# Where the causal mask is added in two attention groups, and how group A's low-order keys are laid out

## The chip, the cores and the metric

The kernel runs as one program on one core of a Trainium2 chip. The core has a matrix engine (TensorE, PE in the profile, with its weight loads as PEld), a vector engine (VectorE, DVE), an activation engine (ScalarE, ACT), GpSimd (POOL) and a queue that starts transfers (SyncE, SP). Each engine works through its own list of instructions in order and waits on semaphores of the others. Matrix products land in PSUM, which the kernel holds as eight tiles of 128 by 512 float32. The metric is device time in microseconds (us), the median of several runs; lower is better.

## The reference

One decoder layer over 512 tokens of width 2048: RMSNorm, one input projection, three token mixers side by side (A: differential attention, B: a gated linear recurrence, C: sparse attention with compressed, selected and window branches), one output projection, then a SwiGLU feed-forward and a last norm. The change touches the scores of A and of two branches of C.

```python
# A: 4 heads, 2 components of 64 dimensions each, causal
s = jnp.einsum('bqhcd,bkhcd->bhcqk', qi, k) * scale
p = masked_softmax(s, kpos[None, :] <= qpos[:, None])
pd = p[:, :, 0] - lam * p[:, :, 1]
...
# C: 6 heads of 128 dimensions; at 512 tokens the selected branch takes every block
s = jnp.einsum('bqgjd,bgqnld->bgjqnl', qi, ksel) * scale
p = masked_softmax(s, mask)
...
s_w = jnp.einsum('bnqgjd,bnkgd->bgjnqk', qw, kwb) * scale
p_w = masked_softmax(s_w, jnp.asarray((dist >= 0) & (dist < WINDOW)))
```

`masked_softmax` puts minus infinity where the mask is false, subtracts the row's maximum, exponentiates and divides by the sum.

## The kernel before

Every float32 operand of a large product is split into a high part rounded to TensorE's fast float32 form ("hi") and the rest ("lo"); a product is then hi·hi + hi·lo + lo·hi, three matrix products into one PSUM tile. ScalarE makes hi (L202) and VectorE makes lo (L203) of each weight tile `w`, from a tile `raw` that SyncE fetched.

The attention runs inside the projections. `tick` counts the time that projection products should take and, each time a set amount has passed (2560 ns during group C, 3840 ns during group A), takes one step of the attention that is queued in a "lane". TensorE's order is exactly the order in which the code is written; the orders of VectorE, ScalarE and GpSimd come from a list scheduler with an estimate of its own. Group C's attention (`c_attention`, 617 to 790 us of the span) lies between projections `paq`, `pak` and `pav`; group A's (`a_attention`, 820 to 925 us) between products `po` of the output projection.

`pipeline` lays the attention out in steps. A step takes one unit: it issues the unit's scores, then the transposes `pt` of the unit before, whose softmax has to be ready by then, then the products with the values of the unit before that. In C a unit is a head, a block of 128 queries and one or two branches (6 units a head, 36 in all); in A it is a head and a block (4 a head, 16 in all), always with both components. Between a unit's scores and its transposes stands one step of projection products, some twelve.

The scores of C are three hi/lo products into a tile `cs` (keys `kh`, `kl`; queries `cqh`, `cql`) and, for each branch, a bfloat16 product of the identity with the mask tile `causal`, which adds a large negative number above the diagonal of the last 128 columns. Then VectorE takes the negated row maximum (`nm`, L916), ScalarE the exponential with its sum (`pr`, `z`, L922), and VectorE the reciprocal and the scaling of `pr` (L925 to L930). In A each component has a tile `as`. Its 64 dimensions are packed so that one product of 128 rows gives hi·hi and lo·hi together: `aqs` holds the query's hi in the component's own 64 rows and its lo in the other 64, `aks` the key's hi twice. The key's lo, `akl`, is one tile for both components, each in its own 64 rows, so the second product has only 64 rows; the third is the mask (all through `mm`, L145). VectorE takes the maximum (L1033), ScalarE the exponential (L1035), and VectorE combines both components (L1037 to L1041).

`a_split(h)` makes these tiles for a head (ScalarE L1001 and L1002, GpSimd L1003, VectorE L1004 and L1005), one head ahead. `at` tiles are a ring of three PSUM tiles, shared by scores, transposes and `finish`, which transposes a finished head of A into `ayp`; a new `at` tile waits until its predecessor three tiles back has been read. `x<-x,po` (L1090) adds a finished column block of the output projection to the residual.

Of the kernel before, what the change touches and what calls it, by code (L numbers as in the profile page):

```python
# [31 lines left out]
F32 = mybir.dt.float32  # L32
F32R = mybir.dt.float32r
BF16 = mybir.dt.bfloat16
I32 = mybir.dt.int32
AF = mybir.ActivationFunctionType
ALU = mybir.AluOpType
# [3 lines left out]
P = 128  # L41
T = 512
# [21 lines left out]
C_MASK = C_D + N_D  # L64
# [43 lines left out]
def tile_hymba(ctx: ExitStack, tc: tile.TileContext, x, attn_norm, w_in, q1, k1, q2, k2, da_norm, hg_norm,  # L108
# [3 lines left out]
    pe, act, dve, pool, sp = nc.tensor, nc.scalar, nc.vector, nc.gpsimd, nc.sync  # L112
# [31 lines left out]
    def mm(o, l, r, start, stop, **kw):  # L144
        return pe.matmul(o, l, r, start=start, stop=stop, **kw)  # L145
# [195 lines left out]
    with ExitStack() as p1:  # L341
# [72 lines left out]
        with tc.manual_schedule(engines=others):  # L414
            g = [pj(f"g1{q}") for q in range(4)]
            for q in range(4):
                mm(g[q], ones, grow[q // 2][:, (q % 2) * 512:(q % 2 + 1) * 512], True, True)

            def take_gain(hf):
                for q in (2 * hf, 2 * hf + 1):  # L420
                    dve.tensor_copy(gain1[:, q * 512:(q + 1) * 512], g[q])

            hn = prepare_x(0, take_gain)
            split_w0(range(12), pool)
            ps0 = [pj(f"pf0{j}") for j in range(2)]
            for tt in range(NT):
                for b in range(4):
                    to_d_major(tt, b, hn, hT)
                if tt == 0:
                    split_w0(range(12, KT), dve)  # L430
                if tt + 1 < NT:
                    hn = prepare_x(tt + 1)
                for k in range(KT):
                    t256_step(ps0, hT, tt, k, w0[k][:, 0], w0[k][:, 1])


            tri_u = cb.tile([P, 2 * P], F32R, name="tri_u")
            dmat = cb.tile([P, N_D], F32R, name="dmat")
            causal = cb.tile([P, P], BF16, name="causal")
            cmpmask = cb.tile([P, NT, 32], F32, name="cmpmask")  # L440
            ident_b = cb.tile([P, P], BF16, name="ident_b")
            lmask = cb.tile([P, 127], I32, name="lmask")
            r = raws.tile([P, 1024], F32, name="draw", tag="raw")
            sp.dma_start(r[:, :N_D], ctab[:, C_D:C_D + N_D])
            dve.tensor_copy(dmat, r[:, :N_D])
            r = raws.tile([P, 1024], F32, name="uraw", tag="raw")
            sp.dma_start(r[:, :2 * P], ctab[:, C_U:C_U + 2 * P])
            sp.dma_start(r[:, 2 * P:3 * P], ctab[:, C_MASK:C_MASK + P])
            sp.dma_start(cmpmask, ctab[:, C_CMP:C_CMP + P].rearrange("p (t n) -> p t n", n=32))
            dve.tensor_copy(tri_u, r[:, :2 * P])  # L450
            dve.tensor_copy(causal, r[:, 2 * P:3 * P])
            dve.tensor_copy(ident_b, ident)
            sp.dma_start(lmask, mtab[:, :])
            pads = cb.tile([P, 2, NT], F32, name="pads")
            sp.dma_start(pads, ctab[:, C_PAD:C_PAD + 2 * NT].rearrange("p (a t) -> p a t", a=2))
            dan = cb.tile([P, 4], F32, name="dan")
            col_load(dan, da_norm, 4)
            dve.tensor_scalar(dan, dan, 1.0 - LAM_INIT, None, op0=ALU.mult)

            r = raws.tile([P, 1024], F32, name="lraw", tag="raw")  # L460
            lq = r[:, :256].rearrange("p (i d) -> p i d", d=64)
            lp = r[:, 256:384].rearrange("p (i d) -> p i d", d=64)
            for i, v in enumerate((q1, k1, q2, k2)):
                sp.dma_start(lq[:, i, :], bcast_row(v, 64))
            le = cb.tile([P, 2], F32, name="le")
            nlam = cb.tile([P, 1], F32, name="nlam")
            for i in range(2):
                dve.tensor_tensor(lp[:, i, :], lq[:, 2 * i, :], lq[:, 2 * i + 1, :], op=ALU.mult)
            dve.tensor_reduce(le, lp, op=ALU.add, axis=AX.X)
            act.activation(le, le, AF.Exp)  # L470
            dve.tensor_tensor(nlam, le[:, 1:2], le[:, 0:1], op=ALU.subtract)
            dve.tensor_scalar(nlam, nlam, LAM_INIT, None, op0=ALU.subtract)
# [364 lines left out]
        def c_attention():  # L837
# [61 lines left out]
            def scores(h, i, bs):  # L899
                g, L, nb = h // 3, (i + 1) * P, len(bs)  # L900
                if i == 2 and bs[0] == 0 and h < 5:
                    prepare(h + 1)
                qh, ql, _ = ready[h]
                qh, ql = qh[:, i * P:(i + 1) * P], ql[:, i * P:(i + 1) * P]
                ps = at(f"cs{h}{i}{bs[0]}")

                sv = ps.rearrange("p (b s) -> p b s", b=nb)[:, :, :L]
                kh = KH[:, bs[0]:bs[-1] + 1, g, :L]
                mm(sv, qh, kh, True, False, skip_group_check=True)
                mm(sv, ql, kh, False, False, skip_group_check=True)  # L910
                for k, b in enumerate(bs):
                    w = max(L, 256)
                    mm(ps[:, 256 * k:256 * k + w], qh, KL[b][:, g, :w], False, False, skip_group_check=True)
                    mm(sv[:, k, L - P:L], ident_b, causal, False, k == nb - 1, skip_group_check=True)
                nm, z, e0 = small(2, "nm"), small(2, "z"), small(1, "e0")
                dve.tensor_reduce(nm[:, :nb], sv, op=ALU.max, axis=AX.X, negate=True)  # L916
                pr = new_pr()
                for k, b in enumerate(bs):
                    if b:
                        dve.tensor_tensor(nm[:, k:k + 1], nm[:, k:k + 1], pads[:, 1, i:i + 1], op=ALU.min)  # L920
                        act.activation(e0, nm[:, k:k + 1], AF.Exp)
                    act.activation(pr[:, k * L:(k + 1) * L], sv[:, k], AF.Exp, bias=nm[:, k:k + 1],  # L922
                                   accum_out=z[:, k:k + 1])
                    if b:
                        dve.scalar_tensor_tensor(z[:, k:k + 1], e0, pads[:, 0, i:i + 1], z[:, k:k + 1],  # L925
                                                 op0=ALU.mult, op1=ALU.add)
                dve.tensor_scalar(z[:, :nb], z[:, :nb], 1e-30, None, op0=ALU.max)
                dve.reciprocal(z[:, :nb], z[:, :nb])
                for k, b in enumerate(bs):
                    dve.tensor_scalar(pr[:, k * L:(k + 1) * L], pr[:, k * L:(k + 1) * L], z[:, k:k + 1],  # L930
                                      gates[:, i, 3 * h + 1 + b:3 * h + 2 + b], op0=ALU.mult, op1=ALU.mult)
                return pr
# [57 lines left out]
        def a_split(h):  # L990


            cols = slice((h % 2) * T, (h % 2 + 1) * T)
            q, k = AQ[h // 2][:, cols], AK[h // 2][:, cols]
            tl = [ysp.tile([P, T], F32R, name=f"{t}{h}", tag=f"y{"bc"[h % 2]}{n}", bufs=1)
                  for n, t in enumerate(("aqs0", "aqs1", "aks0", "aks1", "akl"))]
            kl = tl[4]
            for c in range(2):
                qs, ks = tl[c], tl[2 + c]
                a, b = slice(64 * c, 64 * c + 64), slice(64 - 64 * c, P - 64 * c)  # L1000
                act.activation(qs[a], q[a], AF.Copy)  # L1001
                act.activation(ks[a], k[a], AF.Copy)  # L1002
                pool.tensor_copy(ks[b], ks[a])  # L1003
                dve.tensor_tensor(qs[b], q[a], qs[a].bitcast(F32), op=ALU.subtract)  # L1004
                dve.tensor_tensor(kl[a], k[a], ks[a].bitcast(F32), op=ALU.subtract)  # L1005
            return tl

        a_ready = {}
# [5 lines left out]
        def a_attention():  # L1014
# [4 lines left out]
            def scores(h, i):  # L1019
# [4 lines left out]
                prs, z = [], small(2, "z")  # L1024
                for c in range(2):
                    ps = at(f"as{h}{i}{c}")
                    qc, kc, a = a_ready[h][c], a_ready[h][2 + c], slice(64 * c, 64 * c + 64)
                    n = max(L, 256)
                    mm(ps[:, :n], qc[:, qs], kc[:, :n], True, False)
                    mm(ps[:, :n], qc[a, qs], a_ready[h][4][a, :n], False, False)  # L1030
                    mm(ps[:, L - P:L], ident_b, causal, False, True)
                    nm = small(1, "nm")
                    dve.tensor_reduce(nm, ps[:, :L], op=ALU.max, axis=AX.X, negate=True)  # L1033
                    pr = new_pr()
                    act.activation(pr[:, :L], ps[:, :L], AF.Exp, bias=nm, accum_out=z[:, c:c + 1])  # L1035
                    prs.append(pr)
# [499 lines left out]
```

## Time and profile before

| | us |
|---|---|
| median of 3 runs | 2404.65 (2404.49 to 2404.81) |
| the profiled execution | 2403.6 |
| its span in the trace | 2401.8 |
| TensorE busy | 2361.2 (98%) |
| TensorE's weight loads busy | 2019.1 (84%) |
| VectorE busy | 1584.2 (66%) |
| ScalarE busy | 1032.5 (43%) |
| GpSimd busy | 50.3 (2%) |

The span runs from the first to the last instruction in the trace; the 1.8 us beside it are start and end. Busy times of TensorE overlap, since each product's end is modelled while the next already runs, so the spacing of starts tells what a product costs. Mean granted TensorE clock is 0.997 of full speed.

### The profile page before, as it was taken

To read this page: it belongs to the slowest core of one execution; us is meant where nothing else is said; L and a number is where in the kernel's file an instruction comes from. 1 tells how busy PE (TensorE), PEld (TensorE's weight loads), DVE (VectorE), ACT (ScalarE), POOL (GpSimd) and SP (SyncE) were. 2 spreads that over 40 slices of the span, in tenths; PEclk is the share of its full clock that TensorE was granted. 3 is DMA by queue.
4 is the path that set the end of the run, shared out by engine and by line. 5 is a ranking of instruction groups with operands and counts; after the bars stand their busy time and mean duration, and the time that the engine had idled before them with its cause. 6 is when DMAs were issued, how large, how long until landed. Compare 5 with 4: busy or idle time off the path is not lost.

```text
span 2401.8 us, 32892 instructions
## 1 busy us (share of the span) xinstructions
PE 2361.2 (98%) x12720; PEld 2019.1 (84%) x12720; DVE 1584.2 (66%) x2472; ACT 1032.5 (43%) x1800; POOL 50.3 (2%) x85
## 2 busy tenths in 40 slices
PE   9999999999999999979999999999999999999998
PEld 7898888898888778768888888888888888888887
DVE  6355556543656574687777777777777777777785
ACT  5343443443434443454444444444444444444452
POOL 2000000000000000000000000000000000000001
PEclk9999999999999999999999999999999999999999
DMA  6322222443221422534555555565555555555553
GB/s 207 97 73 80 65 82 81 137 131 100 62 62 53 144 81 74 179 101 122 191 187 190 190 190 193 193 193 193 193 193 193 191 187 188 188 193 192 189 187 150
DMA packets 355888, 354.17 MB, mean 147 GB/s; under 512 B 12882, under 2 KB 286738, under 8 KB 355732
## 3 DMA queue, kind: packets, MB, share of 16 engines
q1 hardware_dynamic: 355732, 352.07, 45.9%
q8 instruction: 100, 1.64, 0.3%
q14 instruction: 56, 0.46, 0.1%
HBM read 302.74 MB, written 49.28 MB: 147 GB/s over the span
## 4 chain that ended last, share of the span: by engine, by line
PE 94%; DVE 3%; ACT 1%; DMA 1%; issue 1%; POOL 0%; SPq 0%; ACTq 0%; POOLq 0%; DVEq 0%
PE fd L145 18%; PE Xu L145 10%; PE Xg L145 10%; PE pig L145 6%; PE po L145 5%; PE Zg L145 5%; PE Zu L145 5%; PE pq L145 3%; PE pf L145 3%; PE pcq L145 3%; PE Vg L145 2%; PE Vu L145 2%; PE bt L145 2%; PE pak L145 2%; PE pk L145 2%; PE sc L145 2%
## 5 line engine op out<-in xcount | busy, mean ns | idle before, releaser
L202 ACT ACTIVATE w<-raw 128x512 fp32r<-128x512 f32 (+2 forms) x698 | 549.0, 790 | 926.7 <-PE fd L145 148.4
L203 DVE TENSOR_TENSOR w<-raw,w 128x512 fp32r<-128x512 f32 (+1 forms) x432 | 293.8, 681 | 343.5 <-ACT w L202 340.4
L145 PE MATMUL fd<-w,aT 128*128 128x512 f32 x1920 | 467.6, 392 | 0.0
L203 DVE TENSOR_TENSOR lo<-raw,w 128x1024 fp32r<-128x1024 f32 x266 | 323.3, 1223 | 179.0 <-ACT w L202 179.0
L145 PEld LDWEIGHTS fd<-w,aT 128*128 128x128 f32 x1920 | 348.9, 188 | 75.3
L1260 DVE TENSOR_TENSOR raw<-raw,raw 128x1024 f32<-128x1024 f32 x134 | 163.4, 1219 | 6.8 <-DMA raw<-in_w_gate_dram 3.2
L145 PE MATMUL pig<-w,hT 128*128 128x512 f32 x576 | 138.3, 395 | 0.0
L145 PE MATMUL po<-w,mT 128*128 128x512 f32 x576 | 136.1, 393 | 0.0
L145 PE MATMUL Xu<-A,w 128*128 128x512 f32 x352 | 125.7, 396 | 1.5 <-DVE C L1346 1.5
L145 PE MATMUL Xg<-A,w 128*128 128x512 f32 x352 | 125.6, 396 | 1.3 <-DVE C L1346 1.3
L145 PE MATMUL Zg<-S,w 128*128 128x512 f32 x352 | 124.2, 392 | 1.7 <-DVE S L1233 1.7
L145 PEld LDWEIGHTS po<-w,mT 128*128 128x128 f32 x576 | 106.8, 188 | 21.5
L145 PEld LDWEIGHTS pig<-w,hT 128*128 128x128 f32 x576 | 106.2, 188 | 21.3
L145 PE MATMUL Zu<-S,w 128*128 128x512 f32 x352 | 124.2, 392 | 0.0
L145 PE MATMUL Xu<-S,w 128*128 128x512 f32 x352 | 123.0, 391 | 0.6 <-ACT C L1343 0.6
L145 PE MATMUL Xg<-S,w 128*128 128x512 f32 x352 | 122.8, 390 | 0.0
L1403 DVE TENSOR_TENSOR xq<-xq,fd 128x512 f32<-128x512 f32 x156 | 100.1, 683 | 0.3
L145 PE MATMUL Xg<-A,lo 128*128 128x256 f32 x352 | 99.1, 281 | 0.0
L145 PE MATMUL Xu<-A,lo 128*128 128x256 f32 x352 | 99.1, 281 | 0.0
L145 PE MATMUL Zg<-S,lo 128*128 128x256 f32 x352 | 98.4, 280 | 0.0
L145 PE MATMUL Zu<-S,lo 128*128 128x256 f32 x352 | 98.4, 280 | 0.0
L145 PE MATMUL Xg<-S,lo 128*128 128x256 f32 x352 | 97.6, 277 | 0.0
(344 smaller groups left out, 4324.8 us busy)
## 6 DMA issues: line engine op xcount, KB each, us to landing
raw<-in_w_gate_dram SPq DMA_DIRECT2D x112, 512.0 KB, 4.6
raw<-in_w_up_dram SPq DMA_DIRECT2D x112, 512.0 KB, 4.6
raw<-in_w_down_dram SPq DMA_DIRECT2D x88, 512.0 KB, 5.2
raw<-in_w_in_dram SPq DMA_DIRECT2D x80, 512.0 KB, 3.5
xq<-y SPq DMA_DIRECT2D x78, 512.0 KB, 4.9
y<-xq SPq DMA_DIRECT2D x78, 512.0 KB, 2.7
raw<-in_w_out_dram SPq DMA_DIRECT2D x32, 512.0 KB, 3.6
raw<-in_w_in_dram SPq DMA_DIRECT2D x48, 256.0 KB, 3.1
```

The lines of the kernel that those rows point to most:

```text
L145: return pe.matmul(o, l, r, start=start, stop=stop, **kw)
L202: act.activation(hi, src, AF.Copy)
L203: dve.tensor_tensor(lo, src, hi.bitcast(F32), op=ALU.subtract)
L1260: dve.tensor_tensor(self.raw[out], self.raw[a], self.raw[b], op=ALU.subtract)
L1403: dve.tensor_tensor(o, o, ps[tt], op=ALU.add)
```

## The change

The mask product goes. In C the three products close the accumulation, and VectorE then adds `causal` (now float32, fetched straight into its tile) to the last 128 columns of each branch in PSUM, one instruction for one or two branches. In A each component gets its own `akl0`, `akl1` of 128 rows, whose other 64 rows GpSimd fills with zeros from a one-column tile, so that the second product has 128 rows; VectorE then adds the mask to the tile of each component. The bfloat16 identity and two conversions at the start of the kernel go.

```diff
-            causal = cb.tile([P, P], BF16, name="causal")
+            causal = cb.tile([P, P], F32, name="causal")
+            zero = cb.tile([P, 1], F32, name="zero")
+            pool.memset(zero, 0.0)
             cmpmask = cb.tile([P, NT, 32], F32, name="cmpmask")
-            ident_b = cb.tile([P, P], BF16, name="ident_b")
...
-            sp.dma_start(r[:, 2 * P:3 * P], ctab[:, C_MASK:C_MASK + P])
+            sp.dma_start(causal, ctab[:, C_MASK:C_MASK + P])
...
-            dve.tensor_copy(causal, r[:, 2 * P:3 * P])
-            dve.tensor_copy(ident_b, ident)
...
                 for k, b in enumerate(bs):
                     w = max(L, 256)
-                    mm(ps[:, 256 * k:256 * k + w], qh, KL[b][:, g, :w], False, False, skip_group_check=True)
-                    mm(sv[:, k, L - P:L], ident_b, causal, False, k == nb - 1, skip_group_check=True)
+                    mm(ps[:, 256 * k:256 * k + w], qh, KL[b][:, g, :w], False, k == nb - 1, skip_group_check=True)
+                own = sv[:, :, L - P:]
+                dve.tensor_tensor(own, own, causal[:, None, :].to_broadcast([P, nb, P]), op=ALU.add)
...
-                  for n, t in enumerate(("aqs0", "aqs1", "aks0", "aks1", "akl"))]
-            kl = tl[4]
+                  for n, t in enumerate(("aqs0", "aqs1", "aks0", "aks1", "akl0", "akl1"))]
             for c in range(2):
-                qs, ks = tl[c], tl[2 + c]
+                qs, ks, kl = tl[c], tl[2 + c], tl[4 + c]
...
                 pool.tensor_copy(ks[b], ks[a])
+                pool.tensor_copy(kl[b], zero[b].to_broadcast([64, T]))
...
-                    mm(ps[:, :n], qc[a, qs], a_ready[h][4][a, :n], False, False)
-                    mm(ps[:, L - P:L], ident_b, causal, False, True)
+                    mm(ps[:, :n], qc[:, qs], kl[:, :n], False, True)
+                    dve.tensor_tensor(ps[:, L - P:L], ps[:, L - P:L], causal, op=ALU.add)
```

TensorE's list is the old one without 80 pairs of weight load and mask product. The scheduled lists of the other engines move too. The first place is VectorE's list in group A at head 0, where block 2 ends and block 3 begins (`as030` is head 0, block 3, component 0; `pr43` holds block 2's weights for the transposes). Before:

```order
L1040 TENSOR_SCALAR pr44_7631<-pr44_7631,z492_7616,nlam_575 128x384
L1041 SCALAR_TENSOR_TENSOR pr43_7623<-pr43_7623,z492_7616,pr44_7631 128x384
L1033 TENSOR_REDUCE nm498_7669<-as030_7665 128x1
L203 TENSOR_TENSOR w514_7840<-raw508_7770,w514_7840 128x512
L1033 TENSOR_REDUCE nm499_7677<-as031_7673 128x1
```

Now:

```order
L1040 TENSOR_SCALAR pr44_7624<-pr44_7624,z492_7609,nlam_574 128x384
L1031 TENSOR_TENSOR as030_7658<-as030_7658,causal_549 128x128
L203 TENSOR_TENSOR w514_7836<-raw508_7763,w514_7836 128x512
L1041 SCALAR_TENSOR_TENSOR pr43_7616<-pr43_7616,z492_7609,pr44_7624 128x384
L1033 TENSOR_REDUCE nm498_7662<-as030_7658 128x1
L1031 TENSOR_TENSOR as031_7666<-as031_7666,causal_549 128x128
```

Block 2's last instruction (L1041) moved behind the mask of block 3 and a weight split. The same happens at head 2, and in group C at the second unit and at the last unit of the fifth head.

The second place is VectorE's list a little further on, where block 3 of head 0 ends and the first column block of the output projection is added to the residual (L1090). Before:

```order
L1040 TENSOR_SCALAR pr46_7679<-pr46_7679,z497_7664,nlam_575 128x512
L1004 TENSOR_TENSOR aqs12_7788<-aq2_6038,aqs12_7788 64x512
L1041 SCALAR_TENSOR_TENSOR pr45_7671<-pr45_7671,z497_7664,pr46_7679 128x512
L1090 TENSOR_TENSOR x1_00_7398<-x1_00_7398,po00_7406 128x512
L1090 TENSOR_TENSOR x1_10_7400<-x1_10_7400,po01_7407 128x512
L1090 TENSOR_TENSOR x1_20_7402<-x1_20_7402,po02_7408 128x512
L1090 TENSOR_TENSOR x1_30_7404<-x1_30_7404,po03_7409 128x512
L203 TENSOR_TENSOR w516_7857<-raw515_7855,w516_7857 128x512
L203 TENSOR_TENSOR w521_7905<-raw515_7855,w521_7905 128x512
```

Now:

```order
L1040 TENSOR_SCALAR pr46_7672<-pr46_7672,z497_7657,nlam_574 128x512
L1090 TENSOR_TENSOR x1_00_7388<-x1_00_7388,po00_7396 128x512
L1090 TENSOR_TENSOR x1_10_7390<-x1_10_7390,po01_7397 128x512
L1090 TENSOR_TENSOR x1_20_7392<-x1_20_7392,po02_7398 128x512
L1090 TENSOR_TENSOR x1_30_7394<-x1_30_7394,po03_7399 128x512
L203 TENSOR_TENSOR w516_7853<-raw515_7851,w516_7853 128x512
L203 TENSOR_TENSOR w521_7901<-raw515_7851,w521_7901 128x512
L1041 SCALAR_TENSOR_TENSOR pr45_7664<-pr45_7664,z497_7657,pr46_7672 128x512
```

Block 3's last instruction moved behind four additions that wait for `po` and two weight splits.

The third place is ScalarE's list at head 1, block 3, ahead of `finish` for head 0 (`aqs`, `aks` are head 2's tiles; `aj` and `aot` read products with the values). Before:

```order
L1001 ACTIVATE aqs03_8042<-aq2_6038 64x512
L1002 ACTIVATE aks03_8044<-ak2_6761 64x512
L1035 ACTIVATE pr53_7927,z522_7920<-as130_7921,nm523_7925 128x512
L1054 ACTIVATE aj11_7949,ass1_7900<-ao1_7898 128x128
L1055 ACTIVATE aot1_7899<-ao1_7898 128x128
L1035 ACTIVATE pr54_7935,z522_7920<-as131_7929,nm524_7933 128x512
```

Now:

```order
L1000 ACTIVATE aqs03_8038<-aq2_6033 64x512
L1001 ACTIVATE aks03_8040<-ak2_6751 64x512
L1000 ACTIVATE aqs13_8039<-aq2_6033 64x512
L1054 ACTIVATE aj11_7945,ass1_7896<-ao1_7894 128x128
L1055 ACTIVATE aot1_7895<-ao1_7894 128x128
L1001 ACTIVATE aks13_8041<-ak2_6751 64x512
L1035 ACTIVATE pr53_7923,z522_7916<-as130_7917,nm523_7921 128x512
```

The exponential of component 0 (`pr53`) moved behind four more instructions.

GpSimd's list gets eight fills of 64 by 512 beside its eight copies of `aks`.

## Rows read from the trace of the kernel before

**Rows 1.** The page: shares of the chain of work that ended last.

```profile
PE 94%; DVE 3%; ACT 1%; DMA 1%; issue 1%; POOL 0%; SPq 0%; ACTq 0%; POOLq 0%; DVEq 0%
```

**Rows 2.** One of the windows: stretch, length, busy PE, PEld, DVE, ACT, POOL, clock, DMA, GB/s.

```profile
760.00:763.40 3.40, 3.40 (x12) 2.72 (x11) 2.38 (x7) 0.52 (x3) 0.00 (x0) 0.50 0.00 0
```

**Rows 3.** TensorE's waits, 610 to 930 us: total us, times, longest.

```profile
PE pt L962 <- DVE pr L930: 4.0, 3, 1.8
...
PEld ayp L1064 <- ACT pr L1035: 0.3, 1, 0.3
```

**Rows 4.** Timeline, group A's first scores: start, us, engine, line, operation.

```profile
820.71 0.28 PE L145 MATMUL as<-aks,aqs 128*128 128x256 f32 x1
...
820.92 0.18 PEld L145 LDWEIGHTS as<-akl,aqs 64*128 64x128 f32 x1 [0.25 <-issue]
820.92 0.38 PE L145 MATMUL as<-akl,aqs 64*128 64x256 f32 x1
...
821.23 0.23 PE L145 MATMUL as<-causal,ident_b 128*128 128x128 bf16 x1
...
821.91 3.02 PE L145 MATMUL po<-w,mT 128*128 128x512 f32 x12
```

**Rows 5.** Timeline, group C: a unit's last block, then the next head's first.

```profile
724.20 0.40 PE L145 MATMUL cs<-kl,cqh 128*128 128x512 f32 x1
...
724.44 0.23 PE L145 MATMUL cs<-causal,ident_b 128*128 128x128 bf16 x1
...
724.50 0.61 PE L962 MATMUL pt<-ident,pr 128*128 128x128 f32 x4
...
728.20 0.55 DVE L930 TENSOR_SCALAR pr<-pr,z,gates 128x512 f32<-128x512 f32 x1
...
728.39 0.19 PEld L145 LDWEIGHTS cs<-kh,cql 128*128 128x128 f32 x1
728.62 0.28 PE L145 MATMUL cs<-kl,cqh 128*128 128x256 f32 x1
...
729.06 0.61 PE L962 MATMUL pt<-ident,pr 128*128 128x128 f32 x4
```

**Rows 6.** VectorE by form: count, busy us, mean ns; idle before.

```profile
L614 DVE TENSOR_TENSOR QS<-sc,ident 128x256 f32<-128x256 f32 x12 | 5.0, 419 | 0.1
L595 DVE TENSOR_TENSOR QS<-KQ,bq 128x256 f32<-128x256 f32 x12 | 5.0, 419 | 0.0
...
L1033 DVE TENSOR_REDUCE nm<-as 128x1 f32<-128x128 f32 x8 | 2.1, 287 | 3.0 <-PE as L145 3.0
```

**Rows 7.** Timeline, group A: block 3 of heads 0 and 1.

```profile
835.79 0.62 DVE L1041 SCALAR_TENSOR_TENSOR pr<-pr,z,pr 128x384 f32<-128x384 f32 x1
836.28 0.40 PE L145 MATMUL as<-aks,aqs 128*128 128x512 f32 x1
...
837.91 0.68 DVE L203 TENSOR_TENSOR w<-raw,w 128x512 fp32r<-128x512 f32 x1
...
837.99 0.50 PE L962 MATMUL pt<-ident,pr 128*128 128x128 f32 x3
...
843.23 2.47 DVE L1090 TENSOR_TENSOR x<-x,po 128x512 f32<-128x512 f32 x4
...
862.65 0.63 ACT L1001 ACTIVATE aqs<-aq 64x512 fp32r<-64x512 f32 x1
...
864.53 0.28 ACT L1054 ACTIVATE aj<-ao 128x128 f32<-128x128 f32 x1
```

**Rows 8.** Timeline, end of C's fifth head.

```profile
757.80 0.90 DVE L930 TENSOR_SCALAR pr<-pr,z,gates 128x512 f32<-128x512 f32 x1
...
758.85 0.63 PE L962 MATMUL pt<-ident,pr 128*128 128x128 f32 x4 [1.82 <-DVE pr L930]
...
760.22 4.50 PE L145 MATMUL pav<-w,hT 128*128 128x512 f32 x12
```

More of the change, by code (lines that the diff above doesn't have):

```diff
@@ L1026, in scores @@
                     ps = at(f"as{h}{i}{c}")
-                    qc, kc, a = a_ready[h][c], a_ready[h][2 + c], slice(64 * c, 64 * c + 64)
+                    qc, kc, kl = a_ready[h][c], a_ready[h][2 + c], a_ready[h][4 + c]
                     n = max(L, 256)
                     mm(ps[:, :n], qc[:, qs], kc[:, :n], True, False)
-                    mm(ps[:, :n], qc[a, qs], a_ready[h][4][a, :n], False, False)
-                    mm(ps[:, L - P:L], ident_b, causal, False, True)
+                    mm(ps[:, :n], qc[:, qs], kl[:, :n], False, True)
+                    dve.tensor_tensor(ps[:, L - P:L], ps[:, L - P:L], causal, op=ALU.add)
                     nm = small(1, "nm")
```

## The prediction, made before the changed kernel ran

> **What bounds the kernel now.** I read the page's chain of work first: 94% of it is TensorE [rows 1], so a product that goes is a gain as long as nothing else becomes late there. Next comes the list of TensorE's waits in the two attention groups [rows 3]: three waits for the weights `pr` in group C, 4.0 us together, and 0.3 us at one `ayp` in group A. So nearly every softmax is ready in time, and the question is by how much. Timelines answer that. VectorE's last instruction of a unit ends .15 us ahead of the product that waits for it (757.80 + .90 = 758.70, product at 758.85) [rows 8]; where more than that lies between, it is spare. At one unit of C it is 728.75 to 729.06, .31 us, of which .16 is spare [rows 5]. Thirteen of C's 36 units have under .6 us between the two. In A the last write is mostly 1.3 to 4 us ahead of the transposes.
>
> The clock belongs to this. The granted clock is half, 1.2 GHz, in one stretch that begins near 760 us, right behind the 1.82 us wait [rows 2, 8]; none follows the other two waits of rows 3. Twelve products take 4.50 us there and 3.02 us at 2.4 GHz [rows 4, 8], so one such stretch costs 1.48 us.
>
> **The products that go.** Spacing of starts is the cost. In A a unit of 256 columns takes 820.71 to 821.91, 1.20 us, for two components; the 64-row product alone holds its start-to-start .31 us (820.92 to 821.23) [rows 4]. Full-row products of 512 in C stand .24 us apart (724.20 to 724.44) [rows 5]; by columns those of 256 stand .12 apart. Four products of 256 are .48 us, so such a unit saves .72. A 512 unit goes from 836.28 to 837.99, 1.71 us [rows 7], and becomes 4 x .24 = .96, saving .75; for 384 I take .74. A: 8 x .72 + 4 x .74 + 4 x .75 = 11.7 us. In C a mask takes .06 us where the transposes follow (724.44 to 724.50) and a two-branch end .44 (728.62 to 729.06), which becomes .24 [rows 5]. C: 24 x .06 + 12 x .20 = 3.8 us. **Gain on TensorE: 15.5 us.**
>
> That a full-row low product runs like C's rests on the load. The load of `kh` is issued at 728.39 and lasts .19, ahead of its product and under the one before [rows 5], while the 64-row load of `akl` starts only with its own product and is marked as .25 us of issue [rows 4]. So I take the load as hidden. [...]
>
> **The added instructions.** No VectorE instruction of the kernel before writes PSUM, so the price of an add is bounded: below by a maximum that reads 128 columns of PSUM, .29, above by a 128x256 addition, .42 [rows 6]. Being nothing or less is excluded, since it stands between products and maximum. I take .29 for 128 columns and .42 for two branches, since an addition out of PSUM and one out of SBUF take the same 419 ns; the ends above are .42 and .55 (a 128x512 scaling [rows 5]). The zero fills lie on an idle GpSimd a head ahead, and the two conversions at the start off the chain: nothing. The float32 mask is ready hundreds of us early: nothing.
>
> **Waits that grow.** Each add sits on the path products, maximum, exponential, scaling, transposes, while TensorE arrives earlier by what it saved.
>
> 1. A, block 2 of heads 0 and 2. The last instruction of block 2 now stands behind block 3's first add, which waits for block 3's own products. From the start S of block 3's scores: second product at S + .24, its end .40 later, add .29, the weight split .68, the instruction itself .62, .15 to the product: S + 2.4. TensorE wants the transposes at S + .96. Before, the instruction was over at 836.41 [rows 7]. Wait 1.4, twice: 2.8 us.
> 2. C, second unit. Its scaling now stands behind the next unit's add, a split, a reciprocal and the next maximum. After TensorE has finished those products (some .2 of tail): .29 + .68 + .29 + half a scaling .28 + .15, with the reciprocal some 2.0 us.
> 3. C, last unit of the fifth head: the wait of 1.82 us grows by the next unit's add .42, its maximum (.42 for 256 columns) and a split .68: 1.5 us.
> 4. A, block 3 of head 0 behind four additions to `x`, which wait for `po`. They take .62 each (2.47 for four) [rows 7]. After the last `po` ends at T: .62 + two splits 1.2 + the instruction .62 + .15, about T + 2.7. TensorE wants it some .4 after T: 2.4 us with .1 allowed for overlap.
> 5. `finish` of head 0: ScalarE's exponential stands behind four more instructions, 2 x .63 + 2 x .28 = 1.8 [rows 7], and the add's .29: 2.1 us. The other `finish` places that come late I take without spare: two of them, add .29 and TensorE's .72, 1.0 each. Less the .3 of before: 3.8 us.
> 6. The rest: thirteen units of C at .3 on average (add .29 to .42, TensorE's .06 to .20, less a spare such as .16) are 4.0; four block-0 and block-2 units of A at .4 are 1.6. Together 5.6 us.
>
> 2.8 + 2.0 + 1.5 + 2.4 + 3.8 + 5.6 = 18.1, against 15.5: **+2.6 us**. So the change shifts the bound from TensorE to the path through VectorE.
>
> **The clock.** Five waits come out at 1.8 us or more; by rows 3, one such wait in two brings a half-clock stretch. I take two more stretches than before, 3.0 us (bounds none to four, 0 to 5.9).
>
> **The sum.** Profiled execution 2403.6 (span 2401.8 and 1.8 beside it) + 2.6 + 3.0 = 2409.2. The median, 2404.65, stands 1.05 above the profiled execution, so 2410.2, rounded to 2410. With the adds at their upper price (.13 more on about twenty path steps) 2.6 more; with no or four stretches 3.0 either way.
>
> **The rivals.** About .2%, 4.8 us, is what a measurement of this kernel can tell from no change: faster ends at 2399.8, slower begins at 2409.5.
>
> First, the waits just eat the gain and no further stretch of half clock comes, as after two of three waits in rows 3: 2403.6 + 2.6 + 1.05 = 2407, the same.
>
> Second, on the other side, the spares of A hold: most units there have 1.3 us and more ahead of the transposes, and an add of .29 with TensorE's .75 needs 1.04. Then terms 5 and 6 fall to some 0 and only the reordered places wait, 8.7 us: 2403.6 - 15.5 + 8.7 + 1.05 = 2398, faster. It decides at whether spares beyond 1.04 us are there at `finish` too. Against it: C's thirteen units, whose spare of .16 is in the rows.
>
> Third, adds at the upper price and four or more stretches: 2403.6 + 2.6 + 2.6 + 5.9 + 1.05 = 2416, slower.
>
> Fourth, the change doesn't do what it says: the full-row load isn't hidden. Each of A's 32 low products would then hold its .18 load [rows 4], 5.8 us: 2410 + 5.8 = 2416. For it: the load beside `akl` isn't hidden now; against it: C's loads of rows 5. [...]
>
> **How the numbers follow.** Forecast (2406 to 2414) .46, of it .18 the same and .28 slower; waits equal the gain .18, the same; spares hold .16, of it .13 faster and .03 the same; dear adds and more stretches .14, slower; load not hidden .06, slower. Faster .13, same .39, slower .48. Range 2398 to 2417: the second rival's lower half and the tail above the third and fourth stay out, some .15.
>
> **What would show it.** In the profile after: two components of 256 columns in .48 us in A; adds of .29 and .42 us; TensorE's waits for `pr` in A where there were none, at blocks 2 and 3 of head 0 and block 2 of head 2, of 1.4 and 2.4 us; a wait at `ayp` near 2 us; in C a wait of 2 us at the second unit and over 3 us at the end of the fifth head; and half-clock stretches behind the longest of these. It is wrong if the waits of TensorE in the two groups sum to under 12 us, if the adds take under .2, or if 64-row and full-row loads cost alike.

## The result, and the profile after

| | before | after |
|---|---|---|
| median | 2404.65 us (7 runs, 2399.21 to 2407.20) | 2419.26 us (7 runs, 2410.12 to 2420.73) |
| the profiled execution, span | 2403.6, 2401.8 | 2419.89, 2418.1 |
| mean granted TensorE clock of that span | 0.997 | 0.991 |
| TensorE busy | 2361.2 (98%) | 2357.4 (97%) |
| VectorE busy | 1584.2 (66%) | 1603.0 (66%) |

The changed kernel is slower: ratio 1.0052, interval 1.0038 to 1.0065. The forecast was 2410, with a range of 2398 to 2417; the side was right, and the median lies 2.3 us above the range and 9.3 above the forecast. The seven runs of before scatter by 8 us; the three ahead of the prediction lay within .4.

The page of after, its chain that ended last, by engine. It answers to [rows 1].

```profile
PE 91%; DVE 5%; ACT 1%; DMA 1%; issue 1%; POOL 1%; SPq 0%; ACTq 0%; POOLq 0%; DVEq 0%
```

Three points of TensorE's share went, two of them to VectorE. TensorE's waits in the two groups, 610 to 940 us (total, times, longest), answer to [rows 3]:

```profile
PE pt L962 <- DVE pr L930: 9.0, 8, 2.9
PE pt L962 <- DVE pr L1041: 6.2, 4, 2.8
PE ayp L1064 <- ACT pr L1035: 3.7, 2, 2.3
PE pt L962 <- DVE nm L920: 3.5, 1, 3.5
```

Before, there were three waits, 4.0 us together. Now these lines have nine in group C, and in group A four for `pr` and two for `ayp`; two more of 0.3 us, one in each group, are put down to ScalarE. The wait put down to `nm` is that of C's fifth head, where VectorE ended `pr` just ahead of that `nm`.

Did TensorE gain what it should? Timeline of after, A's first scores, against [rows 4]:

```profile
830.97 0.28 PE L145 MATMUL as<-aks,aqs 128*128 128x256 f32 x1
830.97 0.19 PEld L145 LDWEIGHTS as<-akl,aqs 128*128 128x128 f32 x1
831.09 0.28 PE L145 MATMUL as<-akl,aqs 128*128 128x256 f32 x1
...
831.32 0.28 PE L145 MATMUL as<-akl,aqs 128*128 128x256 f32 x1
...
831.41 0.53 DVE L1031 TENSOR_TENSOR as<-as,causal 128x128 f32<-128x128 f32 x2 [1.60 <-PE as L145]
831.44 2.93 PE L145 MATMUL po<-w,mT 128*128 128x512 f32 x12
```

It did. The full-row load of `akl` now begins at 830.97, with the product before it, so it is hidden, and the four products take 830.97 to 831.44, .47 us in place of 1.20.

The last view is the clock. These are windows of after around the half-clock stretches in the two groups; the columns are those of [rows 2].

```profile
622.50:629.30 6.80, 5.84 (x15) 4.70 (x16) 3.37 (x12) 1.43 (x7) 0.00 (x0) 0.50 0.25 77
632.80:636.20 3.40, 3.40 (x12) 2.72 (x11) 0.79 (x2) 0.00 (x0) 0.00 (x0) 0.50 0.00 0
765.90:772.70 6.80, 5.68 (x20) 5.04 (x21) 3.54 (x10) 0.76 (x5) 0.69 (x1) 0.50 0.00 0
858.00:861.40 3.40, 3.40 (x12) 2.72 (x11) 1.48 (x5) 0.98 (x7) 0.00 (x0) 0.51 0.31 111
878.50:881.90 3.40, 3.40 (x11) 2.72 (x10) 2.84 (x8) 0.96 (x3) 0.00 (x0) 0.50 0.07 26
929.70:933.10 3.40, 3.40 (x10) 2.66 (x10) 2.20 (x5) 0.75 (x2) 0.00 (x0) 0.50 0.18 70
```

Counting the two of 6.8 us as two each, that is eight stretches of 3.4 us, where before had one [rows 2]. Each begins in a wait of TensorE or at most 1.0 us behind one.

### Where the time went

The table splits the stretch from C's first score to the last `po` product. *Waits* are TensorE's idle gaps of over .1 us. *Scores* is the sum of spacings of the `cs` and `as` products, without waits. *Clock* is, for every product that starts in a half-clock stretch, its spacing less the median spacing of the same pair of products at full clock (1.00). A score inside such a stretch counts in both, so the parts overlap by about 1 us. The kernels k1 to k10 are the experiments below.

| kernel | time | ratio to before | scores | waits | half-clock stretches | clock |
|---|---|---|---|---|---|---|
| before | 2404.65 | | 48.9 | 4.0 | 1 | 1.6 |
| after | 2419.26 | 1.0052 | 34.8 | 23.4 | 8 | 12.0 |
| k1, full rows | 2397.14 | 0.9979 | 39.6 | 6.9 | 1 | 1.6 |
| k2, C's mask | 2410.92 | 1.0039 | 46.2 | 12.0 | 2 | 3.2 |
| k3, A's part | 2407.98 | 1.0026 | 37.3 | 15.2 | 4 | 6.3 |
| k4, no mask | 2395.16 | 0.9967 | 33.3 | 10.3 | 2 | 3.3 |
| k5, five waits filled | 2412.98 | 1.0038 | 34.0 | 15.1 | 3 | 4.8 |
| k6, softmax first | 2413.54 | 1.0044 | 34.5 | 23.5 | 4 | 6.1 |
| k7, softmax first in C | 2414.18 | 1.0046 | 34.2 | 23.9 | 5 | 7.4 |
| k8, rows and softmax first | 2396.02 | 0.9967 | 39.6 | 6.5 | 1 | 1.7 |
| k9, all long waits filled | 2409.64 | 1.0026 | 33.3 | 9.0 | 0 | 0.0 |
| k10, k8 filled | 2397.29 | 0.9970 | 39.1 | 1.7 | 0 | 0.0 |

From before to after the whole stretch went from 356.6 to 371.5 us, +14.9: scores -14.1, waits +19.4, clock +10.4, and -0.8 of overlap and rest. The spans differ by 16.3: .8 was gained ahead of the groups, and 2.2 lost behind them, where waits of the normalization grew (1.7 to 2.7 us at one product) and three half-clock stretches stand in place of two. Each ratio is against runs of before made beside that kernel, whose median was 2402.5 to 2404.7 us, so differences between kernels of the table are surer by the ratios than by the times.

### The profile page after: what moved, and what is told of

It reads as the page before. It is cut to its first block, busy times and chain, and to the rows that moved or that the text cites. A ratio compares the mean times of both kernels' runs of the same rounds, so it can differ in the third digit from the quotient of the medians.

```text
span 2418.1 us, 32816 instructions
## 1 busy us (share of the span) xinstructions
PE 2357.4 (97%) x12640; PEld 2025.0 (84%) x12640; DVE 1603.0 (66%) x2538; ACT 1033.2 (43%) x1800; POOL 58.5 (2%) x94
## 4 chain that ended last, share of the span: by engine, by line
PE 91%; DVE 5%; ACT 1%; DMA 1%; issue 1%; POOL 1%; SPq 0%; ACTq 0%; POOLq 0%; DVEq 0%
PE fd L145 18%; PE Xu L145 10%; PE Xg L145 10%; PE pig L145 5%; PE po L145 5%; PE Zg L145 5%; PE Zu L145 5%; PE pq L145 3%; PE pcq L145 3%; PE Vg L145 2%; PE pf L145 2%; PE Vu L145 2%; PE bt L145 2%; PE pk L145 2%; PE sc L145 2%; PE pak L145 2%
## 5 line engine op out<-in xcount | busy, mean ns | idle before, releaser
L145 PE MATMUL Xu<-S,lo 128*128 128x256 f32 x352 | 98.2, 279 | 0.0
```

## The experiments

The theory after the result: TensorE's gain is there, the waits are about what the prediction summed, and the clock took three times what the prediction gave it. The rivals: one group alone carries the loss; the reordered places carry it; the half-clock stretches have nothing to do with the waits.

### k1: full rows, masks stay on TensorE

```diff
-                    mm(ps[:, :n], qc[a, qs], a_ready[h][4][a, :n], False, False)
+                    mm(ps[:, :n], qc[:, qs], kl[:, :n], False, False)
                     mm(ps[:, L - P:L], ident_b, causal, False, True)
```

> The kernel before with one part of the change: group A's low-order keys as two tiles of 128 rows with zeros; both masks stay products on TensorE. Theory 1 (the forecast's mechanism: TensorE's gain is real, the loss comes from the path through VectorE and the clock): each of 32 components saves about .32 us, 10 us in all; the spares of A cover it, so 2394 to 2396 us, no new wait over .5 us and no half-clock stretch in A. Rival (the full-row load is not hidden, or the zero fills delay something): the start-to-start of the low product stays at .25 to .31 us and the time at 2401 us or more.

Measured: 2397.14 us, ratio 0.9979, interval 0.9970 to 0.9989. TensorE's timeline, A's first scores:

```profile
820.14 0.28 PE L145 MATMUL as<-aks,aqs 128*128 128x256 f32 x1
820.26 0.28 PE L145 MATMUL as<-akl,aqs 128*128 128x256 f32 x1
820.38 0.23 PE L145 MATMUL as<-causal,ident_b 128*128 128x128 bf16 x1
820.42 0.36 PE L145 MATMUL as<-aks,aqs 128*128 128x256 f32 x1
...
820.78 0.94 PE L145 MATMUL po<-w,mT 128*128 128x512 f32 x3
```

Two components take .64 us in place of 1.20. The low product's two spacings fell from .21 and .31 to .12 and .12, and the scores by 9.3 us in all. Its waits rose by 2.9: one of 1.2 us at a unit of A, which the expectation had not allowed, 1.0 together at three `ayp`, and .7 more at a late unit of C. So most of the gain arrives, but the time stays 1.1 us above the 2394 to 2396 expected. This half of the change is good by itself.

### k2 and k3: the masks of one group only

k2 takes the change of the mask in C and leaves A; k3 takes all of A's part and leaves C.

```diff
-                    mm(sv[:, k, L - P:L], ident_b, causal, False, k == nb - 1, skip_group_check=True)
...
+                dve.tensor_tensor(own, own, causal32[:, None, :].to_broadcast([P, nb, P]), op=ALU.add)
```

> The kernel before with only group C's masks moved to VectorE; group A as before. Theory 1: TensorE saves 3.8 us, C's waits grow by the same amount as in the changed kernel (from 4 to some 13 us), and four to five half-clock stretches stand in C instead of one: 2404.65 - 3.8 + 9 + 5 = about 2413 to 2416. Rival (the loss sits in A): 2403 to 2407.

```diff
...
-                    mm(ps[:, L - P:L], ident_b, causal, False, True)
+                    mm(ps[:, :n], qc[:, qs], kl[:, :n], False, True)
+                    dve.tensor_tensor(ps[:, L - P:L], ps[:, L - P:L], causal32, op=ALU.add)
```

> The kernel before with group A's part alone: full-row low-order keys and its mask on VectorE; C as before. Theory 1: TensorE saves 11.7 us, A's waits grow by about 10 us, three half-clock stretches cost 3 to 4 us: 2404 to 2408. Rival (A carries the loss): 2412 or more.

Measured: k2 2410.92 (1.0024 to 1.0054), k3 2407.98 (1.0015 to 1.0036). Both are slower than before, and the two ratios make 1.0065 together, the upper end of after's interval. So neither rival that puts the loss in one group stands. k2's waits grew by 8.0 us, near the 9 expected, and its scores fell by 2.7; it has two half-clock stretches, not the four or five expected, and its time lies below the 2413 to 2416 that went with them. k3 is at the upper end of its 2404 to 2408. k3 stands 11 us above k1, from which it differs by A's mask alone: its scores are 2.3 us less, its waits 8.3 and its clock 4.7 more.

### k4: no mask at all

```diff
-                dve.tensor_tensor(own, own, causal[:, None, :].to_broadcast([P, nb, P]), op=ALU.add)
...
-                    dve.tensor_tensor(ps[:, L - P:L], ps[:, L - P:L], causal, op=ALU.add)
```

> The changed kernel without the two added instructions, so no mask is applied at all (its output leaves out the causal mask). What is left is TensorE's gain with the paths as long as before. Theory 1: 2404.65 - 15.5, some waits back because TensorE arrives earlier (2 to 4 us): 2389 to 2394, and at most two half-clock stretches in the two groups. Rival (the loss is not the added instructions but the reordered lists or the fills): 2405 or more.

Measured: 2395.16, ratio 0.9967 (0.9953 to 0.9981). Scores fell by 15.6 us, just the prediction's 15.5. But the time fell by half of that (7.9 us by the ratio): with no instruction added, waits grew by 6.3 us, since TensorE reached the same softmax earlier, and the clock by 1.7. That is more than the 2 to 4 expected, and the time is 1.2 us above the expected range. By the intervals k4 can't be told from k1, which keeps every mask product: with these orders, most of what the change could gain comes from the full rows, and taking the mask off TensorE adds little even where nothing takes its place. The added instructions and their order cost the rest, 24 us between the medians of k4 and after (20 by the ratios).

### k5 and k9: the waits filled

To separate the wait from the clock, products whose results are overwritten were put ahead of the transposes or of `ayp`. k5 has 83 of them at five places. k9 has 139 at eleven: nine places with 8 to 24 each, one more than its expectation counts, and two with four.

```diff
                     pt = at(f"pt{uid[0]}")
+                    for _ in range(fill.get(a[0], 0)):
+                        mm(pt[:, :256], tri_u[:, :P], tri_u, True, True)
...
```

> The changed kernel with products whose results are overwritten, put on TensorE where it waits longest: 12 to 24 products of 128x256 ahead of the transposes of five places (end of C's fifth head, third unit of the sixth, blocks 2 and 3 of A's head 0, and finish of head 0). Each takes about .12 us, so they fit into the waits and make nothing later. Theory (half-clock stretches follow long waits of TensorE and cost about 1.5 us each beside the wait): the stretches behind these places (about 766, 858 and 878 us) go, some four of 3.4 us, and the time falls by 4 to 6 us, to about 2411 to 2415. Rival (the stretches come with the reorder itself, or cost nothing because TensorE is ahead anyway): no change, 2416 to 2419.

> The changed kernel with overwritten products in every wait of over 1 us in the two groups (eight places, 8 to 24 products of 128x256 each). The second unit's last instruction is in order again by this, so its wait should shrink too. Theory (clock as the missing term): no or one half-clock stretch in the two groups; what is left is TensorE's gain of 14 to 15 us against some 18 us of waits: 2406 to 2410. Rival (the stretches don't depend on idle TensorE): 2413 or more, as with five places filled.

Measured: k5 2412.98 (1.0023 to 1.0053, which overlaps after's interval), k9 2409.64 (1.0016 to 1.0036; after's interval begins at 1.0038). TensorE's timeline of k9 at block 3 of A's head 0, where after waited 2.82 us and a half-clock stretch followed:

```profile
848.23 2.55 PE L145 MATMUL pt<-tri_u 128*128 128x256 f32 x20
851.20 0.66 PE L964 MATMUL pt<-ident,pr 128*128 128x128 f32 x4 [0.42 <-DVE pr L1044]
851.69 0.83 PE L145 MATMUL ao<-av,st 128*128 128x128 f32 x6
852.28 3.00 PE L145 MATMUL po<-w,mT 128*128 128x512 f32 x12
```

The transposes wait for the same `pr` as before, so the path is as long as in after; but the twelve `po` products behind it take 3.00 us. In after the same place reads as follows, with the first ten `po` products:

```profile
857.10 0.63 PE L962 MATMUL pt<-ident,pr 128*128 128x128 f32 x4 [2.82 <-DVE pr L1041]
...
858.26 4.03 PE L145 MATMUL po<-w,mT 128*128 128x512 f32 x10
```

The window from 616 to 940 us, first of k9, then of k5, then of after: the granted clock is the third number from the end.

```profile
616.00:940.00 324.00, 314.96 (x1720) 269.08 (x1720) 217.05 (x545) 142.74 (x379) 23.11 (x29) 1.00 0.25 79
```

```profile
616.00:940.00 324.00, 308.91 (x1650) 262.67 (x1649) 214.14 (x542) 140.55 (x376) 21.51 (x28) 0.98 0.24 77
```

```profile
616.00:940.00 324.00, 300.64 (x1539) 253.04 (x1539) 212.35 (x536) 138.79 (x371) 20.35 (x26) 0.96 0.23 75
```

1.00, .98, .96: none, three and eight stretches. k5 lost five of eight, and its groups took 5.3 us less (366.2 against 371.5), 1.1 each; k9 lost all eight and took 9.6 us less (361.9), 1.2 each, with one instruction of VectorE (second unit of C) back in its old order as a side effect. For k9 that isn't the scatter between executions: all eight of k9 have a mean clock of .996 to .998, all seven of after .990 to .995. k5's four have .994 to .996, so its part in this is weaker.

The products at `finish` of head 0 did not fill its wait. They write the `ayp` tile, which waits for the exponential that reads the tile three back, so they waited too and ran behind. First k5, then k9:

```profile
872.62 2.94 PE L145 MATMUL ayp<-tri_u 128*128 128x256 f32 x15 [2.33 <-ACT pr L1038]
```

```profile
870.69 2.06 PE L145 MATMUL ayp<-tri_u 128*128 128x256 f32 x15 [2.32 <-ACT pr L1038]
```

k9's eight at head 3 and four at C's third unit met no wait at all. So 68 of k5's products and 112 of k9's stood in waits. The two lines also show that a wait alone doesn't decide: behind the same wait, half clock came in k5 (2.94 us for fifteen products) and not in k9 (2.06).

Shown is this much: where a wait before the transposes was filled, no stretch followed, and with nearly all long ones filled the stretches were gone, and their cost with them. Not shown is that each stretch belongs to the wait ahead of it. Two of the five that k5 lost, and two of k9's eight, had stood at waits that stayed as they were: in k5 one of the two at C's first unit (2.88 us) and the one near 929 (1.35), in k9 those at 2.33 and 1.35 us.

With the clock out of the way the prediction's sum is 2403.6 + 2.6 + 1.05, less the one stretch of before, 1.5: 2405.8. k9 lies 3.9 us above it, of which the 27 products outside waits explain 3.3 by their spacing (1.89, .95 and .48).

### k6 and k7: the softmax ahead of other work

```diff
...
+                with tc.high_priority():
+                    own = sv[:, :, L - P:]
+                    dve.tensor_tensor(own, own, causal[:, None, :].to_broadcast([P, nb, P]), op=ALU.add)
...
```

> The changed kernel with the scheduler told that a unit's softmax (mask, maximum, exponential, scaling) goes ahead of other work on VectorE and ScalarE. The four units whose last instruction stood behind the next unit's mask are in order again; one new place (block 3 of A's head 0) stands behind the next unit. Theory 1 (the reordered places carry about 10 us of the waits): waits fall by some 8 us and the clock follows: 2404 to 2410. Rival (the adds on every path carry it): 2412 to 2419.

> The same priority for group C's softmax alone; group A as in the changed kernel. Theory 1: the second unit's wait of 1.9 us and 1.5 of the 3.5 us at the fifth head's end go, and one or two half-clock stretches with them: 4 to 6 us less than the changed kernel, 2411 to 2415. Rival: 2416 to 2419.

Measured: k6 2413.54 (1.0031 to 1.0057), k7 2414.18 (1.0031 to 1.0061). The theory that the reordered places carry some 10 us of the waits fell: the waits are 23.5 and 23.9 us, as in after. k7's time is in its expected range, but not for the expected reason. k6 as the profile lists TensorE's waits:

```profile
PE pt L963 <- DVE pr L931: 9.0, 10, 2.9
PE pt L963 <- DVE pr L1044: 5.5, 4, 4.6
PE pt L963 <- DVE z L929: 4.6, 1, 4.6
```

The second unit's wait shrank from 1.9 to 1.4, and those at block 2 of A's heads 0 and 2 from 1.9 and 1.2 to .3 and .2. But the one at the end of C's fifth head grew from 3.5 to 4.6, and block 3 of A's head 0, now behind the next unit's masks, from 2.8 to 4.6: waits were moved, not removed. The medians lie some 5 us below after (2 by the ratios) and the intervals overlap. In the profiled executions the difference is the clock, since at equal waits k6 has four stretches and after eight; with one execution of each, this can be the scatter between executions.

### k8 and k10: towards a better version

k8 is k1 with the same priority; k10 is k8 with the three waits left in C filled.

> The kernel before with full-row low-order keys in A (masks stay on TensorE) and the priority for both softmax paths. Full rows alone gave 2397.1 with 6.9 us of waits in the two groups. Theory: the waits at C's first unit and fifth head's end shrink and A's 1.2 us wait goes: 2392 to 2396. Rival (the scheduler's order was as good): 2396 to 2399 or more.

> Full-row low-order keys, softmax paths first, masks on TensorE, and overwritten products in the three waits left in C (1.7, 2.2 and 1.2 us). Theory: the one half-clock stretch in C goes, 1.5 us: 2393.5 to 2395.5. Rival: 2396 or more.

Measured: k8 2396.02, ratio 0.9967 (0.9955 to 0.9980); k10 2397.29, ratio 0.9970 (0.9960 to 0.9981). Both are faster than before and after; k8, k10 and k1 can't be told apart by these intervals. In k10 the stretch of half clock in C went as expected and the groups took 1.6 us less than in k8, but a stretch of 6.8 us came behind them, ahead of the normalization, where k8 has none, and the time missed the 2393.5 to 2395.5 expected. Windows of k10:

```profile
616.00:940.00 324.00, 322.15 (x1766) 269.15 (x1765) 204.53 (x485) 142.92 (x383) 21.59 (x28) 1.00 0.26 82
989.60:996.40 6.80, 6.11 (x14) 4.79 (x15) 5.26 (x8) 3.51 (x9) 0.00 (x0) 0.50 0.65 222
```

Just ahead of it TensorE sits idle for 3.60 us before the first `bt` product, in before 1.3. Why it does was not tried.

## Why the prediction was right and wrong

**TensorE's gain: right.** 15.5 forecast. Scores fell by 14.1 in after, with slow-clock products among them, and by 15.6 in k9, where no half-clock stretch is left.

**The load that might not hide: right to discount.** The fourth rival would have had the low product stay at some .3 us; it takes .12 (831.32 to 831.44 us in after, and twice .12 in k1).

**The price of the adds: right.** By form, VectorE in after:

```profile
L1031 DVE TENSOR_TENSOR as<-as,causal 128x128 f32<-128x128 f32 x32 | 8.6, 293 | 13.0 <-PE as L145 13.0
...
L914 DVE TENSOR_TENSOR cs<-cs,causal 128x128 f32<-128x128 f32 x24 | 7.1, 295 | 12.3 <-PE cs L145 12.2
...
L914 DVE TENSOR_TENSOR cs<-cs,causal 128x256 f32<-128x256 f32 x12 | 5.1, 426 | 0.0
```

.29 and .43, taken as .29 and .42 from the rows of a maximum and an addition [rows 6]. In after the means are 293 to 295 ns for 128 columns and 426 ns for 256, with the first source and the destination in PSUM.

**The waits: right in sum, and place by place where a reordered instruction was named; the rest in part by luck.** 18.1 forecast, 19.4 measured.

| place | forecast | after |
|---|---|---|
| A, block 2 of heads 0 and 2 | 1.4 + 1.4 | 1.86 + 1.16 |
| C, second unit | 2.0 | 1.92 |
| C, end of the fifth head | 1.82 + 1.5 | 3.46 |
| A, block 3 of head 0, behind the additions to `x` | 2.4 | 2.82 |
| `finish` of head 0 | 2.1 | 2.33 |
| `finish` of the others | 1.0 + 1.0 | 1.35 |
| the rest, as growth | 5.6 | 5.5 |

The rest is 2.88 - 1.69 at C's first unit, .78 + .31 + .79 + .31 at four units of C, 1.87 - .48 at a late one and .34 twice in A; five short waits, .9 together, are not in the table. The prediction had thirteen units of C at .3 on average and four of A at .4. What came is two large waits in C, a few smaller ones, and .7 us in A, so this term was right in its sum and not in its places. Of the two later `finish` waits only one came. The named places with a reordered instruction stand within .5 us of the forecast. Block 3 of A's head 0 reads as the prediction had it. VectorE's timeline of after:

```profile
852.15 0.55 DVE L1040 TENSOR_SCALAR pr<-pr,z,nlam 128x512 f32<-128x512 f32 x1
852.61 2.47 DVE L1090 TENSOR_TENSOR x<-x,po 128x512 f32<-128x512 f32 x4
855.00 1.28 DVE L203 TENSOR_TENSOR w<-raw,w 128x512 fp32r<-128x512 f32 x2
856.21 0.74 DVE L1041 SCALAR_TENSOR_TENSOR pr<-pr,z,pr 128x512 f32<-128x512 f32 x1
```

Four additions and two splits stand between block 3's scaling and its last instruction; the product that waits for it starts at 857.10.

**The clock: wrong, and this is the step that failed.** The prediction took "two more stretches than before, 3.0 us" for its five waits of 1.8 us or more, because one of before's two such waits, 1.82 and 1.69 us [rows 3], had a half-clock stretch behind it, and bounded them at four. After had seven more, and the clock cost 10.4 us more by spacings: 7.4 of the 9.3 us by which the median missed the forecast. What failed is the number of stretches. Seven waits of 1.8 us or more came, and five of them were followed by half clock, two of those for 6.8 us in place of 3.4; a wait of 1.35 us had one too. The prediction counted each wait as one stretch at most, and those under 1.8 us as none. The price of one, 1.48 us, was right by spacings (12.0 / 8). The prediction's figures in GHz stand for granted clocks of .50 and 1.00; the trace names no frequency. At .50 products of 512 columns start .427 us apart and at 1.00 .228 us (medians, in before as in after). Taking the stretches away gave back 1.2 us each (k9), so of the 7.4 us some 5 are shown by experiment (seven at 1.2, less 3.0); where the difference went is open. Waits 1.3 us above forecast and the stage behind the groups (2.2 us) add to the miss, and 1.7 us come back because the forecast put the median 1.05 above the profiled execution, where after's lies .6 below.

**The range.** The third rival, dear adds with four more stretches, gave 2416; its stretches came, and more of them, but the adds were not dear. With eight waits of a microsecond or more in its own list, one of which had its stretch before, the prediction had ground to let seven more come for the upper end: 2403.6 + 2.6 + 7 x 1.48 + 1.05 = 2417.6. That still lies below the median; the double stretches are in no row of before.

What stays open is which wait brings a stretch, and so how many come. Its length alone doesn't tell: in after a wait of 1.35 us (near 928) had one behind it, waits of 1.86 (847) and 1.87 (790) had none. The same wait goes either way: that of 1.35 us has none behind it in k3, k5, k6, k7 and k9, and that of 2.88 us at C's first unit has one in k5 and k7, two in after and none in k2 and k6 (2.85 and 2.88 us). The number isn't fixed by the kernel either. After's shortest execution took 2410.12 us, the forecast, at a mean clock of .995 against .991 in the profiled one; by an estimate from these two clocks it had five or six stretches fewer (.004 x 2408 us, at 1.7 us of lost clock for a stretch of 3.4).

## What to carry to other kernels

An engine that was 98% busy didn't sell its instructions at their spacing here: without any added work, k4 got back half of the 15.6 us that it removed, because the softmax behind it became the limit. Added instructions of .29 to .43 us, on that path in each of 52 units, cost more here than the products they replaced, although VectorE was busy for only 66%. And where TensorE's idle gaps grow, price each gap twice: its length, and a half-clock stretch behind it at the price that the kernel's own rows show, with as many stretches as gaps for the upper end; two gaps here even brought two each.

## What the runs showed that was not expected

- The granted clock differed from execution to execution of the same kernel, and the time went with it. Of after's seven executions the shortest, 2410.12 us, has a mean clock of .995, and the four longest, 2419.26 to 2420.73, have .990 or .991. All seven are executions of one kernel, so its profile is one draw of several.
- Products without any use made a kernel shorter: k9 runs 139 products more than after, 112 of them in waits, and is about 10 us ahead of it by the medians (6 by the ratios).
- A 64-row product cost more than a 128-row one of the same columns: .31 us to the next product in place of .12, with its load .25 us late [rows 4]. Zeros in the other 64 rows were worth 9.3 us over 32 products (k1).
